# S5's tables with both parts side by side, modulation's loads first, the filters' second half later

## The chip, the core and the metric

The kernel runs on one core of a Trainium2 chip. Its engines work side by side and each in its own order: TensorE (PE) multiplies matrices, VectorE (DVE) and ScalarE (ACT) work element by element, GpSimd (POOL) gathers, SyncE (SP) issues most of the loads. The metric is the time of one execution on the device, in microseconds (us). Before the change it is 1788.65 us, the median of three runs (1786.26 to 1789.34).

## What is computed

One layer over 512 latent tokens of width 1024 and 256 tokens of context. A conditioning vector gives shifts, scales and gates (modulation). The normalised and modulated tokens go through one projection whose columns are split: 512 of them to S5 (32 groups of 16 channels, a complex diagonal state space in both directions, whose scans over the latents start from the context's last states), 1536 to Hyena (three streams, a convolution of width 3, and two long convolutions through spectra with filters that a small network makes). Both halves are joined and projected, and a retrieval of single-neuron experts (PEER) ends the layer.

```python
px = modulate(rmsnorm(x, g_norm1[l]), shx1, scx1) @ w_in[l] + b_in[l]
pc = modulate(rmsnorm(ctx, g_norm1[l]), shc1, scc1) @ w_in[l] + b_in[l]
...
lam_bar, b_bar = s5_discretise(...)            # b_bar = ((lam_bar - 1) / lam) * b
st_c = s5_states(uc, lam_bar, b_bar, None, dr == 1)
st_x = s5_states(ux, lam_bar, b_bar, h0, dr == 1)
y_x = y_x + s5_readout(st_x, s5_c_re[l, dr], s5_c_im[l, dr])
...
filt_x = hyena_filters(L, hf_w1, hf_b1, hf_wh, hf_bh, hf_freq, hf_wout, hf_decay)
z_x = hyena_mixer(px[..., S5_W:], hy_conv_w, hy_conv_b, filt_x, hy_d, rows)
mix_x = merge_head_groups(y_x, z_x, w_glu, b_glu, g_out_s5, g_out_hy, w_out)
x = x + gx1 * mix_x
x = x + gx2 * peer(modulate(rmsnorm(x, g_norm2), shx2, scx2), ...)
```

## The kernel before

The program is written as a sequence of stages for the Tile framework, whose scheduler then sets the order of the instructions on each engine; an engine runs its list strictly in that order. Two strings give the order in which the stages are written. EARLY orders the first loads on SyncE's queue: `h`, `f`, `s` are small tables, `w`, `t`, `d` the filters' output weights, the tables of sines and cosines and the decay rates, `x` the rows of x and of the context, `a0` to `a7` the eight blocks (1 MB each) of modulation's weights, `b` the S5 parameters. SEQ orders the work: `H` the filters' hidden layers, `A0` to `A3` (`filter_rows`, lines 507 to 534) the four filter groups, `B` their sums (536), `N` their norms (555), `k` and `K` their spectra (`filter_spectra`, 568), which go to the DRAM tile KD; `P0` to `P7` the products with modulation's weights (pmod, 426) and `M` the vectors made of them (modr, 431), `S` the norms of the rows of x, `X` and `C` the modulated x (xs, 443 to 446) and context; `U` and `u` the first four blocks of the projection for x and for the context (`s5_inputs`, `s5_context`, 653 and 665); `5` the S5 parameters (many small VectorE operations, most of 128x32). A product of two fp32 matrices is made of three matmuls of halves (lines 307 to 309), and the lower half of each block of weights (win0l to win15l, 303) is a subtraction of 128x1024 on VectorE.

After these comes S5 itself, in eight slices of four groups (SEQ has ended there). For each slice `added` (908) makes W, the input weights as complex products of powers (PB) and bb; turns them on TensorE (wt, WT, 930), and multiplies them with the inputs Ur (pv, VS). `states` (946) makes the turns E (586), turns VS by E (rt, VP), scans along time (H, 974) and turns back (ru, SF); `from_states` (993) makes C, the output weights, and multiplies SF by it (py, 1010). The complex product of two tables takes four multiplications, an addition and a subtraction, all through the helper at line 586. Hyena is written between the second and the third slice: projection blocks win4 to win15 with their convolutions (hq, uq, x2t), the spectra of the inputs (pu, pw, 1161, multiplied into spt and sp, 1163 to 1168), and back (pE, pY), until the inverse roots rz (487). Then the GLU, the output projection, the norms, and PEER.

Memory is held in pools. The filters and the S5 parameters share one pool (`ff`, line 340), which is closed when SEQ has ended (873); the pool of S5's slices (`fb`, 877) opens then and takes its place, so that a first write there waits for the last read of what lay there. In PSUM the tag of `ps5` has three banks, shared by the spectra of the filters (two banks a group), by wt, pv and py. The tag `sp` has four buffers, in which the filters' output weights and the tables trig lie, and later the spectra of the inputs.

## Time and profile before

| what | us |
|---|---|
| median of three runs | 1788.65 |
| the profiled execution | 1782.07 |
| its span | 1780.3 |
| TensorE busy in the span | 1670.0 (94%) |
| VectorE busy | 1491.0 (84%) |
| ScalarE busy | 817.9 (46%) |
| first matmul of the projection (px, win0) | 89.49 |
| first S5 row on VectorE (wt1w) | 162.24 |
| first product of the input spectra on VectorE (spt) | 280.99 |
| transposes behind the inverse roots (pyt) | 400.34 |
| first matmul of PEER's queries (pq) | 477.84 |

All times are counted from the start of the span. An engine that is idle is not by that the one to blame: what matters is which of them others wait for, and that differs from stretch to stretch.

### The profile page before, as it was taken

The page shows a single profiled execution, that of the slowest core. Times are in us where ns is not written, and L with a number is a line of the kernel's source. Part 1 is how long each engine was busy: PE and PEld are TensorE (multiplying, and loading weights), DVE is VectorE, ACT ScalarE, POOL GpSimd, SP SyncE. Part 2 cuts the span into 40 slices and gives each one's busy share as a digit, 9 for nine tenths or more (in the row PEclk, how much of TensorE's full clock was granted, in tenths as well). Part 3 has the DMA queues.
Part 4 walks back from the last instruction along what each step waited for, and adds up shares of the span by engine and source line. Part 5 has one row for each costly group of instructions (what it writes and reads, how often), then busy time and mean ns, then how long its engine had stood idle before and what let it go on. Part 6 is the DMA issues. An engine that isn't in the chain of part 4 may idle for free.

```text
span 1780.3 us, 24942 instructions
## 1 busy us (share of the span) xinstructions
PE 1670.0 (94%) x8731; PEld 1410.6 (79%) x8731; DVE 1491.0 (84%) x3039; ACT 817.9 (46%) x1616; POOL 169.5 (10%) x158
## 2 busy tenths in 40 slices
PE   5799998789899999998999989999999999999997
PEld 1477654456799999998999978877878788999996
DVE  7965989986688989989999958788878787888887
ACT  3443543234433323236989844444434344444444
POOL 0000000000000000001101101111111112222221
PEclk9899999899899999999999989999999999999999
DMA  9436453122444444446989899999999998999981
GB/s 372 155 98 209 156 170 91 51 75 71 124 156 139 141 147 151 145 147 246 330 319 333 322 321 387 385 356 378 363 353 358 357 339 320 342 327 349 335 311 71
DMA packets 170228, 436.13 MB, mean 245 GB/s; under 512 B 17139, under 2 KB 102004, under 8 KB 150902
## 3 DMA queue, kind: packets, MB, share of 16 engines
q1 hardware_dynamic: 128854, 251.28, 41.8%
q0 software_dynamic: 18432, 134.23, 20.5%
q10 hardware_dynamic: 22816, 49.03, 7.6%
q8 instruction: 69, 1.13, 0.3%
q14 instruction: 57, 0.47, 0.1%
HBM read 381.52 MB, written 52.92 MB: 244 GB/s over the span
## 4 chain that ended last, share of the span: by engine, by line
PE 63%; DVE 12%; issue 1%; ACT 1%; DMA 1%; ACTq 0%; DVEq 0%
PE pacc L308 9%; PE pacc L309 9%; PE pacc L307 9%; PE pa L309 7%; PE pa L307 7%; PE pa L308 7%; PE pgg L1566 5%; PE pq L309 2%; PE pq L307 2%; PE pq L308 2%; DVE idx L1352 1%; DVE rs L1350 1%; PE pg L1266 1%; DVE idx L1348 1%; PE po L307 1%
## 5 line engine op out<-in xcount | busy, mean ns | idle before, releaser
L308 PE MATMUL pacc<-vl,wwh 128*128 128x512 f32 x768 | 299.6, 391 | 1.8 <-DVE vl L1607 1.8
L309 PE MATMUL pacc<-vh,wwl 128*128 128x512 f32 x768 | 295.1, 390 | 0.0
L1430 POOL DMA_INDIRECT uvr<-in_uv_dram,gidx x128 | 157.1, 1228 | 1090.6 <-DVE accg L1439 764.6
L307 PE MATMUL pacc<-vh,wwh 128*128 128x512 f32 x768 | 238.3, 391 | 8.4 <-ACT vh L1606 8.4
L1607 DVE TENSOR_TENSOR vl<-vr,vh 128x1024 fp32r<-128x1024 f32 x128 | 155.3, 1219 | 26.8 <-ACT vh L1606 26.7
L307 PEld LDWEIGHTS pacc<-vh,wwh 128*128 128x128 f32 x768 | 143.5, 188 | 39.4 <-ACT vh L1606 11.3
L308 PEld LDWEIGHTS pacc<-vl,wwh 128*128 128x128 f32 x768 | 144.1, 188 | 33.6 <-DVE vl L1607 3.6
L309 PEld LDWEIGHTS pacc<-vh,wwl 128*128 128x128 f32 x768 | 144.2, 188 | 29.7
L1439 DVE SCALAR_TENSOR_TENSOR accg<-uvr,wgt,accg 128x1024 f32<-128x1024 f32 x128 | 163.7, 1279 | 4.1 <-ACT wgt L1436 1.8
L1431 DVE SCALAR_TENSOR_TENSOR junk<-uvr,hrow 128x1024 f32<-128x1024 f32 x128 | 155.9, 1218 | 0.0
L1606 ACT ACTIVATE vh<-vr 128x1024 fp32r<-128x1024 f32 x128 | 133.0, 1050 | 44.1 <-PE pacc L309 33.8
L1615 ACT ACTIVATE wwh<-gw 128x384 fp32r<-128x384 f32 x128 | 67.1, 524 | 185.4 <-PE pacc L308 146.1
L1616 DVE TENSOR_TENSOR wwl<-gw,wwh 128x384 fp32r<-128x384 f32 x128 | 70.9, 554 | 53.9 <-ACT wwh L1615 53.9
L1566 PE MATMUL pgg<-o,o 128*128 128x128 f32 x768 | 93.0, 278 | 4.3 <-ACT o L1562 4.3
L1566 PEld LDWEIGHTS pgg<-o,o 128*128 128x128 f32 x768 | 92.1, 194 | 4.5 <-ACT o L1562 4.5
L1557 DVE TENSOR_TENSOR o<-iotak,cols 128x512 f32<-128x512 f32 x96 | 65.8, 685 | 10.1 <-PE pgg L1566 10.1
L1564 DVE TENSOR_SCALAR o<-iotak,cols 128x128 f32<-128x128 f32 x240 | 70.1, 342 | 0.0
L1434 ACT ACTIVATE wgt<-dots 128x1 f32<-128x1 f32 x128 | 25.3, 198 | 93.1 <-DVE junk L1431 93.1
L1562 ACT ACTIVATE o<-o,cols 128x128 f32<-128x128 f32 x144 | 63.6, 493 | 0.0
L1369 ACT ACTIVATE ga<-pa 128x384 f32<-128x384 f32 x128 | 60.4, 472 | 2.4 <-DVE gw L1612 2.1
L1568 ACT ACTIVATE gst<-pgg 128x512 f32<-128x512 f32 x96 | 56.7, 591 | 1.2 <-PE pgg L1566 1.1
L1612 DVE TENSOR_TENSOR gw<-gal,gc 128x384 f32<-128x384 f32 x88 | 48.4, 553 | 7.4 <-DMA gal<-GA 5.5
(1812 smaller groups left out, 4133.9 us busy)
## 6 DMA issues: line engine op xcount, KB each, us to landing
vr<-in_uv_dram SPq DMA_DIRECT2D x128, 512.0 KB
GD<-gst ACTq DMA_DIRECT2D x12, 2048.0 KB
gc<-GD SPq DMA_DIRECT2D x32, 768.0 KB
GA<-ga ACTq DMA_DIRECT2D x88, 192.0 KB
gal<-GA SPq DMA_DIRECT2D x88, 192.0 KB
wb<-in_w_ada_dram SPq DMA_DIRECT2D x32, 512.0 KB
wa<-in_w_ada_dram SPq DMA_DIRECT2D x8, 1024.0 KB
KD<-kk SPq DMA_DIRECT2D x16, 256.0 KB
```

Source lines behind the costliest of these rows:

```text
L307: nc.tensor.matmul(o, a[0], b[0], start=start, stop=False)
L308: nc.tensor.matmul(o, a[0], b[1], start=False, stop=False)
L309: nc.tensor.matmul(o, a[1], b[0], start=False, stop=stop_)
L1430: GP.indirect_dma_start(out=uvr, out_offset=None, in_=I["uv"], in_offset=bass.IndirectOffsetOnAxis(ap=gidx[:, s:s + 1], axis=0))
L1431: ins = V.scalar_tensor_tensor(junk, uvr[:, 0:D], 1.0, hrow, ALU.mult, ALU.mult, accum_out=dots[:, s:s + 1])
L1439: V.scalar_tensor_tensor(accg, uvr[:, D:2 * D], wgt[:, s:s + 1], accg, ALU.mult, ALU.add)
L1564: last = V.tensor_scalar(o1[:, e], iotak, cols[:, 0, t:t + 1], cols[:, 2, t:t + 1], ALU.is_equal, ALU.mult)
L1566: mm = PE.matmul(pg[:, e, :], o2[:, e], o1[:, e], start=True, stop=True)
L1606: A.activation(vh, vr, AF.Copy)
L1607: (V if QUIET or i >= P - VLV else GP).tensor_tensor(vl, vr, vh.bitcast(F32), ALU.subtract)
L1615: A.activation(wh, gw, AF.Copy)
L1616: last = V.tensor_tensor(wl, gw, wh.bitcast(F32), ALU.subtract)
```

## The change

Two strings change, four groups of tables, and the pools.

- EARLY: the small tables, then modulation's weights, with the S5 parameters behind `a2` and x behind `a3`; the filters' tables and decay rates behind `a7`.
- SEQ: the S5 parameters first, then modulation's products one behind the other, `M`, and the first filter group; the spectra of the second order of the filters (k2, k3, K2, K3), before the context's `U3`, now end the sequence. A new part `W` writes W of slices 0 and 1 and E of slice 0 there.
- Tables: b, c and the finer factor of E are kept as (-im, re, im) or (im, re, -im) side by side. A complex product then is one multiplication of the real part of the powers by two neighbouring parts, one of the imaginary part by the two before, and one addition, each twice as wide. c comes so from the host; for b and E three negations on ScalarE make the third part. H is made in place of VP.
- Pools: the filters' pool lies on the right side, the parameters' pool apart from it, closed by `W`; S5's early tables (W, CM, the temporaries q2) take that one's place, and the main ones (VS, R, E, rt, SF, C, WT, YC) that of the filters' pool. WT of slices 0 and 1 and E of slice 0 take buffers of the tag `sp`.

What the diff changes in `columns` and `gates_r` stands behind RGATE, which is 0 in both programs.

```diff
@@ -53,8 +53,8 @@
-EARLY = "h f s t1 t0 x1 x0 w0 a0 d0 a1 a2 w1 a3 a4 a5 d1 a6 a7 x2 b d2 d3"
-SEQ = "H P0 S0 A0 P1 B0 k0 P2 A1 P3 B1 P4 P5 P6 P7 M X0 N0 k1 S2 K0 X1 K1 U0 C0 A2 B2 U1 C1 5 u0 u1 A3 U2 u2 B3 N1 k3 k2 K3 U3 K2 u3"
+EARLY = "h f s a0 a1 a2 b a3 x1 x0 a4 a5 a6 a7 t1 w0 d0 t0 w1 d1 x2 d2 d3"
+SEQ = "H 5 P0 P1 P2 S0 P3 P4 P5 P6 P7 M A0 X0 B0 X1 A1 S2 k0 B1 N0 k1 K0 C0 U0 K1 C1 U1 A2 u0 u1 B2 A3 W U2 B3 u2 N1 U3 u3 k2 k3 K2 K3"
@@ -339,19 +338,24 @@
-    fpool = ff.enter_context(tc.tile_pool(name="ff", bufs=1))
+    fpool = ff.enter_context(tc.tile_pool(name="fl", bufs=1, side="right"))
+    fe_ = ExitStack()
+    epool = fe_.enter_context(tc.tile_pool(name="fe", bufs=1))
@@ -671,6 +676,147 @@
+    b3 = sm("b3", [P, G5, 3, 16])
+    EB3 = sm("EB3", [P, G5, 3, 8])
...
+    def both_parts(o, pw, x3, g0, name):
+
+        t = (q2(name + "1"), q2(name + "2"))
+        for e in range(2):
+            tt(t[e], pw[e][:, :, g0:g0 + GS].rearrange("p j g -> p g j").unsqueeze(3).broadcast_to((P, GS, T8, 32)),
+               x3[:, g0:g0 + GS, 1 - e:3 - e].rearrange("p g e h -> p g (e h)").unsqueeze(2).broadcast_to((P, GS, T8, 32)), ALU.mult)
+        tt(o.rearrange("p e g j h -> p (g j) e h"), *(x.rearrange("p g j (e h) -> p (g j) e h", h=16) for x in t), ALU.add)
...
+        WT = sm(f"WT{s_}", [P, 2, GS, P], tag="sp", bufs=4) if s_ < NEARLY else sl(f"WT{s_}", [P, 2, GS, P], tag="WT", bufs=1)
...
+        for e in range(2):
+            tt(t[e].rearrange("p (g a n) -> p g a n", g=GS, n=16), EA_[e][:, gs].unsqueeze(3).broadcast_to((P, GS, A8, 16)),
+               EB3[:, gs, 1 - e:3 - e].rearrange("p g e b -> p g (e b)").unsqueeze(2).broadcast_to((P, GS, A8, 16)), ALU.mult)
+        tt(E.rearrange("p e g (a b) -> p (g a) e b", b=8), *(x.rearrange("p (q e b) -> p q e b", e=2, b=8) for x in t), ALU.add)
...
+        H, t2 = v3(f"H{s_}", "rt", 2), v3(f"rt2{s_}", "rt", 2)
+        tt(H, VS, both(E[:, 0]), ALU.mult)
+        tt(t2, VS, both(E[:, 1]), ALU.mult)
+        tt(H[:, 0], H[:, 0], t2[:, 1], ALU.add)
+        tt(H[:, 1], H[:, 1], t2[:, 0], ALU.subtract)
@@ -712,6 +858,14 @@
+        elif part[0] == "W":
+            fe_.close()
+            fb_ = ExitStack()
+            pools5[0] = fb_.enter_context(tc.tile_pool(name="fb1", bufs=1))
+            for s_ in range(NEARLY):
+                weights(s_)
+                if s_ < NEARLY - 1:
+                    turns(s_)
@@ -853,17 +1003,17 @@
+            cmul((b3[:, :, 1], b3[:, :, 2]), (bc_h(fr_), bc_h(fi_)), (gh(bre), gh(bim)), (gh(bt1), gh(bt2)))
+            for x in (b3, c3):
+                A.activation(*((x[:, :, 0], x[:, :, 2]) if x is b3 else (x[:, :, 2], x[:, :, 2])), AF.Copy, scale=-1.0)
@@ -873,151 +1023,18 @@
+    pools5[1] = fb_.enter_context(tc.tile_pool(name="fb2", bufs=1, side="right"))
...
-        t1, t2 = q2(f"ct1{s_}"), q2(f"ct2{s_}")
-        pr, pi = (pw4(x, g0, GS) for x in PC)
-        cr, ci = (x4(gh(cre[:, e]), g0, GS) for e in range(2))
-        tt(t1, pr, cr, ALU.mult)
-        tt(t2, pi, ci, ALU.mult)
-        tt(C[0], t1, t2, ALU.add, FG)
-        tt(t1, pi, cr, ALU.mult)
-        tt(t2, pr, ci, ALU.mult)
-        tt(C[1], t1, t2, ALU.subtract, FG)
```

What this does to the order, first on TensorE at the last two groups of the filters' spectra (pke and pko, from hfb). Before, they end where the projection block win4 begins:

```order
L576 MATMUL pke_1206<-hfb_1034,trig_97 128x256 x4
L576 MATMUL pko_1207<-hfb_1034,trig_97 128x256 x4
L576 MATMUL pke_1256<-hfb_632,trig_97 128x256 x4
L308 MATMUL pc_1274<-cs_601,win3h 128x256
L309 MATMUL pc_1274<-cs_601,win3l 128x256
L307 MATMUL pc_1274<-cs_601,win3h 128x256
L308 MATMUL pc_1274<-cs_601,win3h 128x256
L309 MATMUL pc_1274<-cs_601,win3l 128x256
L307 MATMUL px_1681<-xs_412,win4h 128x512
L576 MATMUL pko_1257<-hfb_632,trig_97 128x256 x4
L308 MATMUL px_1681<-xs_414,win4h 128x512
L309 MATMUL px_1681<-xs_412,win4l 128x512
```

After, the last two (from hfb_901 and hfb_1040) stand behind the whole of win8, and the first pv of S5 right behind them:

```order
L307 MATMUL px_1885<-xs_540,win8h 128x512
L308 MATMUL px_1885<-xs_538,win8l 128x512
L581 MATMUL pke_1372<-hfb_901,trig_100 128x256 x4
L581 MATMUL pko_1373<-hfb_901,trig_100 128x256 x4
L581 MATMUL pke_1390<-hfb_1040,trig_100 128x256 x4
L1152 MATMUL pz_1854<-ident,uq_1851 128x128 x4
L439 MATMUL modr0T<-ident,modr_1868 128x98 x2
L581 MATMUL pko_1391<-hfb_1040,trig_100 128x256 x4
L439 MATMUL modr0T<-ident,modr_1868 128x98 x2
L646 MATMUL pmodr_1925<-wb_0_0_1927,sc 1x512 x2
L764 MATMUL pv_1422<-Ur,WT_1106 128x96 x4
L764 MATMUL pv_1430<-Ur,WT_1106 128x96 x4
```

What moved: five blocks of the projection, with their convolutions' transposes (pz) and the later modulation (pmodr), from behind the last spectrum to ahead of it.

A little ahead of that on TensorE in the changed program stands the second of the four groups (pke_1354 and pko_1355, from hfb_1039), whose two halves are set apart by 14 rows of the projection; the copies WT of slice 1 on ScalarE come behind the last reads of trig_101 by this group:

```order
L583 ACTIVATE kev_1364<-pke_1354 128x512
L1155 ACTIVATE uw<-pz_1800 128x4x128
L1139 ACTIVATE hp_1845<-px_1820,small 128x512
L1141 ACTIVATE hq_1847<-px_1820,cbq,small 128x512
L738 ACTIVATE WT_1150<-wt_1151 128x512
L738 ACTIVATE WT_1150<-wt_1157 128x512
L301 ACTIVATE win9h<-win9r 128x1024
L1139 ACTIVATE hp_1910<-px_1885,small 128x512
L1141 ACTIVATE hq_1912<-px_1885,cbq,small 128x512
L583 ACTIVATE kev_1382<-pke_1372 128x512
L583 ACTIVATE kev_1400<-pke_1390 128x512
```

On VectorE, the place where S5 begins. Before, W of slice 0 (wt1w) follows the last rows of the spectra (kk):

```order
L581 TENSOR_TENSOR kk_1218<-kev_1216,pko_1207 128x512
L581 TENSOR_TENSOR kk_1221<-kev_1216,pko_1207 128x512
L303 TENSOR_TENSOR win5l<-win5r,win5h 128x1024
L581 TENSOR_TENSOR kk_1268<-kev_1266,pko_1257 128x512
L581 TENSOR_TENSOR kk_1271<-kev_1266,pko_1257 128x512
L586 TENSOR_TENSOR wt1w_1332<-PB_868,bb 128x512
L586 TENSOR_TENSOR wt2w_1333<-PB_869,bb 128x512
L586 TENSOR_TENSOR wt1w_1391<-PB_868,bb 128x512
L586 TENSOR_TENSOR wt2w_1392<-PB_869,bb 128x512
L586 TENSOR_TENSOR et_1449<-EA_880,EB_882 128x384
L586 TENSOR_TENSOR et_1449<-EA_881,EB_883 128x384
L586 TENSOR_TENSOR WBrw_1330<-wt1w_1332,wt2w_1333 128x512
```

After, the last kk are followed by C and H of slice 0; W, E and the products ct for C have been made earlier:

```order
L1148 TENSOR_TENSOR uq_1916<-hq_1912 128x256
L1149 TENSOR_TENSOR uq_1916<-hq_1912 128x256
L586 TENSOR_TENSOR kk_1384<-kev_1382,pko_1373 128x512
L586 TENSOR_TENSOR kk_1387<-kev_1382,pko_1373 128x512
L586 TENSOR_TENSOR kk_1402<-kev_1400,pko_1391 128x512
L586 TENSOR_TENSOR kk_1405<-kev_1400,pko_1391 128x512
L651 TENSOR_TENSOR mod<-modr0T,small 128x4 x4
L591 TENSOR_TENSOR C_1455<-ct_1456,ct_1457 128x32x2x16
L591 TENSOR_TENSOR H_1464<-VS_1421,E_1119 128x768
L591 TENSOR_TENSOR rt_1465<-VS_1421,E_1119 128x768
L591 TENSOR_TENSOR H_1464<-H_1464,rt_1465 128x384 x2
L302 TENSOR_TENSOR win10l<-win10r,win10h 128x1024
```

What moved: 34 rows of VectorE's list more stand ahead of the first S5 row that the filters' memory holds back, among them W of two slices, E of one, and four more blocks win.

## Rows read from the trace of the kernel before

**Rows 1.** Busy time of each engine by stretch; columns in its first line.

```profile
core 0: us, PE busy (x) PEld busy (x) DVE busy (x) ACT busy (x) POOL busy (x), PEclk, DMA share, GB/s
0.00:50.00 50.00, 29.66 (x120) 12.30 (x120) 38.98 (x182) 17.90 (x38) 0.70 (x6) 0.93 0.90 348
50.00:89.49 39.49, 29.57 (x150) 15.70 (x149) 37.95 (x91) 17.58 (x31) 0.00 (x0) 0.91 0.49 154
89.49:162.24 72.75, 70.59 (x374) 57.24 (x372) 36.48 (x67) 28.75 (x46) 0.00 (x0) 0.98 0.42 127
162.24:280.99 118.75, 111.97 (x639) 72.78 (x636) 107.86 (x189) 59.13 (x124) 1.95 (x10) 0.99 0.55 177
280.99:400.34 119.35, 95.08 (x483) 56.29 (x481) 113.46 (x197) 35.32 (x84) 1.23 (x6) 0.93 0.24 63
400.34:477.84 77.50, 69.05 (x289) 49.82 (x289) 52.23 (x73) 36.81 (x62) 0.95 (x1) 0.90 0.38 112
477.84:1780.00 1302.16, 1264.05 (x6687) 1146.42 (x6687) 1104.02 (x2245) 622.45 (x1232) 164.64 (x135) 0.99 0.79 281
```

**Rows 2.** Chain of waits, 369 to 400 us: start, length, what.

```profile
369.54 0.94 DVE H L974
...
376.01 3.72 PE pY L1189 x16
...
384.42 3.47 PE pY L1189 x16
...
394.88 0.70 DVE x2t L1195
...
400.34 1.13 PE pyt L1227 x4
```

**Rows 3.** VectorE in order of time, 340 to 350 us: start, length, operation.

```profile
340.87 0.95 DVE L586 TENSOR_TENSOR rt<-VS,E 128x768 f32<-128x768 f32 x1
341.73 0.68 DVE L586 TENSOR_TENSOR wt1w<-PB,bb 128x512 f32<-128x512 f32 x1
342.34 0.68 DVE L586 TENSOR_TENSOR wt2w<-PB,bb 128x512 f32<-128x512 f32 x1
342.94 0.68 DVE L1163 TENSOR_TENSOR spt<-pu,sp 128x512 f32<-128x512 f32 x1
...
348.59 0.99 DVE L586 TENSOR_TENSOR et<-EA,EB 128x384 f32<-128x384 f32 x2
349.50 0.68 DVE L1167 TENSOR_TENSOR sp<-spt,spt 128x512 f32<-128x512 f32 x1
```

**Rows 4.** Loads of wa: shortest/median/longest ns, first and last start in us.

```profile
L360 SPq DMA_DIRECT2D wa<-in_w_ada_dram x8: 328/328/762, 4.8 to 28.5; - x8
```

**Rows 5.** Copy of pmod and first load's row on VectorE, in order of time.

```profile
8.40 0.18 DVE L600 TENSOR_SCALAR ex<-small 128x32 f32<-128x32 f32 x1 [5.89 <-DMA small<-in_small_dram]
...
55.36 0.68 DVE L431 COPY modr<-pmod 98x512 f32<-98x512 f32 x1
```

**Rows 6.** TensorE in order of time at three places.

```profile
89.49 0.58 PE L307 MATMUL px<-xs,win0h 128*128 128x512 f32 x1
...
154.78 1.67 PE L576 MATMUL pko<-hfb,trig 128*128 128x256 f32 x7
...
156.75 0.39 PE L307 MATMUL px<-xs,win4h 128*128 128x512 f32 x1
156.98 0.40 PE L308 MATMUL px<-xs,win4h 128*128 128x512 f32 x1
...
278.97 1.55 PE L1161 MATMUL pu<-uw,fwd 128*128 128x512 f32 x3 [1.29 <-DMA fwd<-in_fwd_dram]
```

**Rows 7.** VectorE in order of time, 155 to 163 us.

```profile
155.55 1.23 DVE L303 TENSOR_TENSOR win5l<-win5r,win5h 128x1024 fp32r<-128x1024 f32 x1 [2.01 <-ACT win5h L302]
156.70 1.28 DVE L581 TENSOR_TENSOR kk<-kev,pko 128x512 f32<-128x512 f32 x2
162.24 0.69 DVE L586 TENSOR_TENSOR wt1w<-PB,bb 128x512 f32<-128x512 f32 x1 [4.27 <-DMA KD<-kk]
```

**Rows 8.** VectorE's waits, 86 to 163 us: total, times, longest.

```profile
DVE win4l L303 <- ACT win4h L302: 8.5, 1, 8.5
DVE kk L581 <- issue: 6.2, 1, 6.2
DVE wt1w L586 <- DMA KD<-kk: 4.3, 1, 4.3
```

**Rows 9.** VectorE in order of time at 281 us.

```profile
280.99 0.69 DVE L1163 TENSOR_TENSOR spt<-pu,sp 128x512 f32<-128x512 f32 x1 [1.39 <-PE pu L1161]
```

More of the change, by code (lines that the diff above doesn't have):

```diff
@@ L65 @@
 NYU = 2
-NW = 2
+NEARLY = 2
 NF4 = 4
@@ L97 @@
 NOO = 3
-S5M = 1
 HYAT = 2
@@ L384, in build @@
         elif what[0] == "b":
-            for e, t in enumerate((bre, bim, cre)):
-                early(t, I["bc"][:, e] if e < 2 else I["bc"][:, 2:4])
+            for e, t in enumerate((bre, bim)):
+                early(t, I["bc"][:, e])
+            early(c3, I["c3"])
         elif what[0] == "w":
```

284 lines of the change are left out of this document (139 added, 145 removed).

## The prediction, made before the changed kernel ran

> **What bounds the kernel now.** I read the busy time of the engines in stretches first [rows 1], with the cuts at the places where the kernel changes hands. The last stretch, from the first product of the queries at 477.84 us to the end, is 1302 of the 1780.3 us; the change touches nothing that lives there (its edits of the gates stand behind a switch that is off in both programs). What can move the time is when that stretch begins. Ahead of it lie six stretches: VectorE is nearly full in the second (37.95 of 39.49 us), has half of the third to spare (36.48 of 72.75), while TensorE is full there (70.59), is full again in the fourth (107.86 of 118.75) and above all in the fifth (113.46 of 119.35, TensorE at 95.08). The chain of waits [rows 2] says the same of the fifth: it goes back over H, the products of the spectra and the pY matmuls, alternately VectorE and TensorE, to the inverse square roots behind which the GLU starts at 400.34. From 400.34 to 477.84 both programs have one order of instructions, so I carry those 77.5 us over unchanged. The question is thus: when does that row at 400.34 come?
>
> **Loads first.** Before, the eight blocks of modulation's weights are issued up to 28.5 us, behind the filters' tables, and the copy of the finished sums stands at 55.4 [rows 4, 5]. After, twelve megabytes (8.4 of the weights, 2.1 of x, 1.3 of S5's parameters, the small table) stand ahead of or at the last block. At the 348 GB/s of the first 50 us [rows 1] that is 34.5 us, plus the 8.4 us at which the first load frees VectorE [rows 5]: the copy comes at about 43, some 12 us sooner. Little of it arrives at the first projection (89.49) [rows 6], because VectorE is in the way: what it must do before that projection is the same list in both orders, less 0.3 us (the S5 parameters and W of slice 0 take the place of two filter groups), it was busy 76.9 us in the first 89.5 [rows 1], and it can't start before 8.4. That allows no earlier than 84 to 85. And the filters' decay rates now land behind the weights, at about 46; ScalarE's row that takes their absolute value stands ahead of the rows that modulate x, so these begin at 46 too and not at 43, with 36.6 us of VectorE's list still to run, and some waits for TensorE's transposes. I take 86.5 (84 to 91): a gain of 3.
>
> **Tables with both parts side by side.** A table of W or C cost six operations of 128x512 and costs three of 128x1024; one of E six of 128x384 and now three of 128x768. On a full VectorE what counts is the distance from start to start, not the shown duration: 0.60 for 128x512, 0.46 for 128x384, 0.86 for 128x768 [rows 3], 1.15 for 128x1024 [rows 7]. So a table of W or C falls from 3.60 to 3.45, one of E from 2.76 to 2.58, about 0.2 each with the unrounded starts; 24 tables make 4.7 us. The shown durations (0.68 and 1.23) would give more, 0.13 a pair. [...] The three negations added go to ScalarE, which is half idle there (17.58 of 39.49).
>
> **The filters' second half moved back.** This is the edit that costs. TensorE's rows between the first projection and the last spectrum were worth 63.1 us by the spacing of their kinds, and took 66.6 (89.49 to about 156.1, where the last one starts) [rows 6]. In the new order the last spectrum stands behind 119 more matmuls of the projections (0.23 each, 27.1), 14 more of the later modulation (4.9), 12 more of the spectra's own (5.2; these stood ahead of the first projection), W's edges and transposes for two slices with those of the first convolutions (5.2), and a little else: 105.9. With the same factor of 1.055 they take 111.7, to 198.2.
>
> This matters because the pool of S5's main tables (VS, R, SF, C, H) takes the memory of the filters' pool. Before, the first S5 row on VectorE waits 4.3 us for the last write of the filters' results to DRAM and starts at 162.24, six behind the start of the last spectrum [rows 6, 7]. After, the same wait stands ahead of C and H of slice 0: 198.2 + 6 = 204.2, and about 2 more, because H waits for VS, which ScalarE can only copy then. I take 206, against 162.24. Against that stands what now lies ahead of it: W of slices 0 and 1 (6.8), E (2.6), ct (2.3), four more splits of projection weights (4.5), five groups of short convolutions (9.7), the rest small: 27.2 us of VectorE's list. So VectorE does 36.5 + 27.2 = 64 us in the 119 from 86.5 to 206 and idles 55; before it idled 36 in the third stretch, mostly behind TensorE and the write [rows 8]. The moved work fills half of what the later start opens.
>
> **From there to the first product of the spectra** (280.99 [rows 9]) VectorE's list falls from 106.4 to 61.6. Before, 106.4 took 118.75, a factor of 1.116, with TensorE's 104.1 in step beside it. After, TensorE's list is 63.1 against 61.6, as evenly matched, so I keep the factor: 68.7, to 274.7. Without any loss it is 268, with the 1.18 that TensorE shows there (104.1 in the 122.9 to 278.97 [rows 6]) 279.
>
> **From there to the inverse roots** VectorE's list was 111.6 and took 119.35 (1.069). After, only three slices' states are done by then, and not four, which leaves 124.4 (the saving of the tables is in it). At a factor of 1.05 that is 130.6, to 405.3; with 1.013 and 1.069 on either side, 126 and 133. So the 6 us gained up to the first product are spent, and more: the work done early is less than the slice that moved behind.
>
> **The sum.** 405.3 against 400.34 is 5 us later. On the profiled execution (1782.07, span 1780.3) that is 1787; that execution lies 6.6 below the median of the runs shown, 1788.65, to which I add the difference: 1794. A difference of about 0.2% (3.6 us) is what a measurement of this kernel can tell from none.
>
> **Rivals.** *A gapless S5 (faster).* W, E and C of the first slices are ready when the filters end, so S5 could run without the waits of the fourth stretch. First projection at 84, last spectrum at 195.7, S5 at 201.7, 61.6 x 1.02 to 264.5, 124.4 x 1.013 to 390.5: 10 sooner, 1779. For it: in the fifth stretch VectorE loses only 6 of 119. Against: TensorE has 63.1 of its own in that stretch, and the two feed each other. It decides from a first product of the spectra before 268. *The edits cancel.* Projection at 85, the tables save the shown durations (0.13 a pair, 72 pairs, 9.4 us, so 4.7 more than I count), or the factor in the fourth stretch is 1.05: 400 +- 3.5, thus 1789. [...] *A late end of the filters (slower).* The second half's spectra are chained: the transposes of W of slice 1 wait in two of the three PSUM banks of their tag until ScalarE may copy them, which by the order it does only behind the second of the four groups (their memory is a trig table's until then), so the first two groups have one bank for their two halves, and go TensorE, ScalarE, TensorE, VectorE in turn. If one of those turns is late, TensorE stands with the projections behind it. At 6 us for each of the two (VectorE's longest wait ahead of kk is 6.2 in [rows 8]) S5 starts at 218, and with 68.7 and 133 behind it the roots come at 420: +19, 1808. *That the change doesn't do what it says:* the loads are in fact reordered in the program, so only its effect on the first projection can fail; it is in the 84 to 91.
>
> **How the numbers follow.** Forecast (+5, its own range +1 to +12): 0.42. Cancels (-3.5 to +3.5): 0.23. Gapless: 0.20. Late filters: 0.15. Of the forecast's 0.42 some 0.12 lies within 3.6 us of no change, of the gapless case 0.02, and 0.04 of the cancelling case falls out on the fast side. That gives faster 0.22, same 0.33, slower 0.45. The range of eight in ten reaches into the gapless case (-7) and into the late one (+17): 1782 to 1806.
>
> **What would show it.** In the changed profile: the copy of modulation's sums at about 43 (if it is at 50 or later, the loads are not what I think); the first projection at 84 to 91; the last sum of the spectra on VectorE at about 200, and C and H of slice 0 right behind a wait for the write to DRAM at 202 to 208, with VectorE under 60% busy from 90 to there; the first product of the spectra at 270 to 279; the row at 400.34 at 400 to 410; and the queries 77.5 behind it. Consecutive 128x1024 rows of W and C should start 1.15 apart. I would be wrong if S5's first H came well before the last spectrum (then the memory is not what it waits for), or if VectorE had no idle time between 90 and 200.

## The result, and the profile after

The changed kernel takes 1805.08 us (median of four runs, 1803.64 to 1807.4), the kernel before 1787.45 on the same chip: 1.0108 of it, with a 95% interval of 1.0091 to 1.0126. By the ratio that is 19 us more; the two medians lie 17.6 us apart. The profiled execution took 1804.69 us, its span is 1802.9. The time lies within the range that was given (1782 to 1806), at its upper end; the forecast itself, 5 us slower, was too small by a factor of almost four.

The busy time by stretch in the profile after, cut at the rows that [rows 1] is cut at (columns in the first line); the fourth cut is the first S5 row that waits for the filters' memory:

```profile
core 0: us, PE busy (x) PEld busy (x) DVE busy (x) ACT busy (x) POOL busy (x), PEclk, DMA share, GB/s
0.00:50.00 50.00, 25.64 (x118) 5.74 (x119) 41.62 (x205) 12.92 (x28) 0.70 (x6) 0.83 0.89 348
50.00:99.47 49.47, 40.69 (x128) 20.51 (x128) 40.34 (x71) 26.77 (x52) 0.31 (x1) 0.62 0.40 128
99.47:215.40 115.93, 115.05 (x637) 89.42 (x636) 61.58 (x106) 46.21 (x80) 0.62 (x2) 1.00 0.47 148
215.40:284.60 69.20, 64.79 (x354) 41.29 (x353) 62.56 (x83) 37.04 (x74) 0.74 (x5) 1.00 0.58 196
284.60:419.77 135.17, 102.76 (x527) 63.77 (x525) 126.21 (x190) 39.25 (x95) 1.58 (x8) 0.89 0.22 53
419.77:498.09 78.32, 67.45 (x289) 48.74 (x289) 52.35 (x74) 36.69 (x62) 0.95 (x1) 0.94 0.37 111
498.09:1802.90 1304.81, 1263.28 (x6688) 1145.08 (x6687) 1105.14 (x2245) 624.18 (x1232) 165.96 (x135) 0.99 0.80 281
```

From the inverse roots to the queries it is 78.3 us (77.5 before), behind them 1304.8 (1302.2): 3 of the 22.6 us by which the two spans differ. The other 19.4 are there when the row at 400.34 in [rows 1] comes at 419.77. Up to it VectorE was busy 332 us (334.7 before) and idle 87 (65.6 before). The loss is idle time of VectorE: 5 us more of it ahead of the first projection, 18 more between that and the first S5 rows, where TensorE is full (115.05 of 115.93) as in the third stretch of [rows 1], 4 less from there to the first product of the spectra, and 3 more behind that.

What the prediction had not seen stands ahead of the first projection. TensorE in order of time in the profile after (start, length, operation, in brackets the idle time before it and what ended it):

```profile
64.92 3.14 PE L646 MATMUL pmodr<-wb,sc 128*1 128x512 f32 x8 [2.43 <-DMA wb<-in_w_ada_dram]
68.00 2.07 PE L526 MATMUL pf<-hwo,hid 64*128 64x256 f32 x4
...
73.52 1.87 PE L646 MATMUL pmodr<-wb,sc 128*1 128x512 f32 x4 [1.24 <-DMA wb<-in_w_ada_dram]
...
83.08 1.87 PE L646 MATMUL pmodr<-wb,sc 128*1 128x512 f32 x4 [2.93 <-DMA wb<-in_w_ada_dram]
...
90.65 3.11 PE L581 MATMUL pke<-hfb,trig 128*128 128x256 f32 x8
...
96.12 1.97 PE L581 MATMUL pke<-hfb,trig 128*128 128x256 f32 x8
...
99.47 0.58 PE L306 MATMUL px<-xs,win0h 128*128 128x512 f32 x1
```

The last modulated block of x starts at 70.8 us (88.2 before), but the first projection starts at 99.47 (89.49 before [rows 6]). In between TensorE works down its list: the later modulation, which waits four times for its weights (6.9 us in all), the filters' products pf, and two groups of spectra. The same eight pke take 3.11 us at 90.65 and 1.97 at 96.12: the granted clock is 0.62 from 50 to 99.5. In the 50 us ahead of that it is 0.83 (0.93 before [rows 1]), and there TensorE was busy 25.64 us (29.66 before) and waited 10.1 us for modulation's weights.

The later modulation and its waits are not what is new there: in the kernel before, 28 rows of it (32 after) stand ahead of the first projection too, and wait 8.3 us for their loads. New is what the rows take. Everything up to the first projection, before and then after:

```profile
0.00:89.49 89.49, 59.23 (x269) 28.00 (x269) 76.93 (x272) 35.48 (x69) 0.70 (x6) 0.92 0.72 262
0.00:99.47 99.47, 66.34 (x244) 26.24 (x245) 81.96 (x275) 39.69 (x79) 1.02 (x7) 0.73 0.65 238
```

TensorE has 25 rows fewer and is busy 7 us longer, at a granted clock of 0.73 and not 0.92. With the mean time that each kind of row took before, the list after would take 54 us (an estimate, with cT counted as xT); the 12 us above that go with the lower clock.

Where S5 begins, VectorE in order of time:

```profile
207.23 1.29 DVE L586 TENSOR_TENSOR kk<-kev,pko 128x512 f32<-128x512 f32 x2 [2.14 <-PE pko L581]
208.43 0.36 DVE L651 TENSOR_TENSOR mod<-modr0T,small 128x4 f32<-128x4 f32 x4
215.39 1.23 DVE L591 TENSOR_TENSOR C<-ct,ct 128x1024 f32<-128x1024 f32 x1 [6.59 <-DMA KD<-kk]
217.63 0.96 DVE L591 TENSOR_TENSOR H<-VS,E 128x768 f32<-128x768 f32 x1 [1.02 <-ACT VS L769]
```

This is [rows 7] fifty-three us later: the wait for the write to DRAM is there, 6.6 and not 4.3 us, and behind it the short one for VS.

### The profile page after: what moved, and what is told of

Read it like the earlier page. It is cut to its first block, busy times and chain, and to the rows that moved or that the text cites. A ratio compares the mean times of both kernels' runs of the same rounds, so it can differ in the third digit from the quotient of the medians.

```text
span 1802.9 us, 24884 instructions
## 1 busy us (share of the span) xinstructions
PE 1679.7 (93%) x8731; PEld 1414.5 (78%) x8731; DVE 1489.8 (83%) x2967; ACT 823.1 (46%) x1620; POOL 170.9 (9%) x158
## 4 chain that ended last, share of the span: by engine, by line
PE 62%; DVE 11%; DMA 1%; issue 1%; ACT 1%; ACTq 0%; DVEq 0%; SPq 0%
PE pacc L307 10%; PE pacc L308 9%; PE pacc L306 9%; PE pa L308 7%; PE pa L306 7%; PE pa L307 7%; PE pgg L1578 5%; PE pq L308 2%; PE pq L306 2%; PE pq L307 2%; DVE idx L1370 1%; DVE rs L1368 1%; PE pg L1284 1%; DVE idx L1366 1%; DVE val L1365 1%
## 5 line engine op out<-in xcount | busy, mean ns | idle before, releaser
L1448 POOL DMA_INDIRECT uvr<-in_uv_dram,gidx x128 | 158.4, 1238 | 1090.3 <-DVE accg L1457 744.4
L306 PE MATMUL pacc<-vh,wwh 128*128 128x512 f32 x768 | 243.4, 391 | 10.8 <-ACT vh L1621 10.8
L1457 DVE SCALAR_TENSOR_TENSOR accg<-uvr,wgt,accg 128x1024 f32<-128x1024 f32 x128 | 163.7, 1279 | 5.3 <-ACT wgt L1454 3.3
```

The lines of the kernel that those rows point to most:

```text
L306: nc.tensor.matmul(o, a[0], b[0], start=start, stop=False)
L1448: GP.indirect_dma_start(out=uvr, out_offset=None, in_=I["uv"], in_offset=bass.IndirectOffsetOnAxis(ap=gidx[:, s:s + 1], axis=0))
L1457: V.scalar_tensor_tensor(accg, uvr[:, D:2 * D], wgt[:, s:s + 1], accg, ALU.mult, ALU.add)
```

## The experiments

The table has all runs, with the profiles' times: the first projection, the last sum of the filters' spectra (kk), the first product of the input spectra (spt), VectorE's idle time up to that, its busy time from there to the inverse roots, and the inverse roots (rz on VectorE, which starts within 0.1 us of the row at 400.34 in [rows 1]; that row is a transpose that starts with the roots and not behind them). Ratios are to the kernel before, on the same chip each. A profile is one execution: e11 and e17 are the same kernel, and their columns up to spt differ by 3 to 5 us, while from spt to the roots both take 114.9.

| run | ratio, interval | projection | last kk | spt | idle to spt | busy behind | roots |
|---|---|---|---|---|---|---|---|
| before | 1 | 89.5 | 157.3 | 281.0 | 59.7 | 113.4 | 400.3 |
| changed | 1.0108 (1.0091 to 1.0126) | 99.5 | 207.8 | 284.6 | 78.5 | 126.3 | 419.9 |
| e1 old loads and stages | 1.0097 (1.0070 to 1.0124) | 97.0 | 190.4 | 291.7 | 74.1 | 114.5 | 414.8 |
| e2 old loads | 1.0056 (1.0036 to 1.0077) | 108.6 | 196.2 | 279.3 | 69.5 | 121.4 | 410.8 |
| e3 one W early | 1.0045 (1.0029 to 1.0061) | 99.5 | 181.6 | 288.3 | 66.7 | 110.0 | 410.1 |
| e4 later modulation late | 1.0132 (1.0107 to 1.0157) | 87.5 | 200.5 | 298.5 | 76.4 | 111.1 | 421.1 |
| e5 tables alone | 1.0022 (1.0011 to 1.0033) | 85.6 | 158.4 | 281.0 | 58.9 | 109.4 | 404.2 |
| e6 e1 with one W early | 1.0006 (0.9991 to 1.0021) | 96.5 | 161.8 | 284.4 | 51.9 | 99.2 | 393.4 |
| e7 new order, one pool, none early | 1.0058 (1.0037 to 1.0080) | 95.3 | 167.3 | 282.6 | 65.9 | 115.5 | 408.6 |
| e8 none early | 1.0068 (1.0045 to 1.0091) | 99.8 | 180.8 | 289.2 | 71.0 | 113.5 | 414.3 |
| e9 two W early, no E | 1.0088 (1.0064 to 1.0113) | 99.4 | 186.3 | 291.8 | 73.0 | 113.4 | 416.8 |
| e10 one W and E early | 1.0104 (1.0080 to 1.0128) | 99.2 | 187.0 | 290.0 | 72.2 | 114.0 | 417.0 |
| e11 e2 with one W early | 0.9993 (0.9979 to 1.0007) | 103.5 | 169.0 | 282.6 | 55.8 | 103.5 | 397.5 |
| e12 e1 with one W and E early | 1.0011 (0.9997 to 1.0025) | 98.1 | 163.7 | 287.3 | 54.5 | 99.4 | 398.3 |
| e13 e3 with idle matmuls | 1.0046 (1.0032 to 1.0061) | 103.5 | 181.4 | 288.5 | 67.9 | 111.6 | 408.2 |
| e14 changed with idle matmuls | 1.0128 (1.0106 to 1.0150) | 95.4 | 209.3 | 288.2 | 81.3 | 126.1 | 426.0 |
| e15 e11 with idle matmuls | 1.0047 (1.0033 to 1.0062) | 111.3 | 177.2 | 288.7 | 61.4 | 104.0 | 404.0 |
| e16 e3 with mixed loads | 1.0023 (1.0013 to 1.0032) | 103.0 | 173.2 | 279.5 | 60.3 | 112.2 | 403.1 |
| e17 e11 again | 0.9983 (0.9971 to 0.9996) | 107.7 | 173.7 | 286.2 | 59.3 | 103.5 | 401.1 |

**The order of loads and stages put back (e1).** The theory after the result was still the prediction's: the order moves the filters' second half, and that costs.

```diff
-EARLY = "h f s a0 a1 a2 b a3 x1 x0 a4 a5 a6 a7 t1 w0 d0 t0 w1 d1 x2 d2 d3"
-SEQ = "H 5 P0 ... B2 A3 W U2 B3 u2 N1 U3 u3 k2 k3 K2 K3"
+EARLY = "h f s t1 t0 x1 x0 w0 a0 d0 a1 a2 w1 a3 a4 a5 d1 a6 a7 x2 b d2 d3"
+SEQ = "H P0 S0 A0 ... u0 u1 A3 W U2 u2 B3 N1 k3 k2 K3 U3 K2 u3"
```

> The changed kernel with the two strings of before (loads and stages in the old order; the early W stands behind the last filter group), tables and pools as changed. If the order of loads and stages is what costs, nearly all of the 19 us comes back and the narrower tables' 4 to 5 us show: 1782 to 1787, first projection at 88 to 91. If the pools are what costs (S5's main tables in the filters' memory, WT in the buffers of the trig tables), it stays at 1795 or above, with S5's first C behind the write to DRAM later than 185 us.

1803.07 us: both strings back, and hardly anything is won. The filters end at 190 here, against 157 before, so it is not the strings alone that put their second half behind the projections. The theory fell.

**The loads alone put back (e2).** Only the EARLY line of e1.

> The changed kernel with the old order of the first loads alone (the filters' tables ahead of modulation's weights), stages, tables and pools as changed. If the late filter tables are what holds the first projection at 99.5 us, it comes at 89 to 92 and the time falls by 7 to 10, to about 1796. If TensorE's rows of the later modulation hold it (16 of them stand ahead of it in this order too), it stays at 97 or later and the time within 4 us of 1805.

1796.26, 9 us won, but not by the way that was expected: the first projection comes later still (108.6), with more of the filters done ahead of it: the scheduler lays out TensorE's order anew with EARLY, and 20 rows of pf and 32 of the spectra more stand there.

**One slice early (e3).**

```diff
-NEARLY = 2
+NEARLY = 1
```

> The changed kernel with only slice 0's W early (W of slice 1 and E of slice 0 come later, so no second WT waits for the buffer of a trig table). In the order the last spectrum of the filters then stands behind 125 matmuls of the projections and not 216. If that wait is what moves the filters' end, the last sum of the spectra comes at about 180 and not 208, S5's C at 187, and the time falls by 5 to 12, to 1793 to 1800. If VectorE's whole list decides, what is taken out of the idle time comes back behind it and the time stays within 4 us of 1805.

1793.88, 11 us won, with the first projection where it was (99.5). The filters end at 181.6. Busy times of e3 from the first projection to the last sum, to the spectra's first product, to the roots:

```profile
99.50:182.30 82.80, 81.92 (x452) 65.88 (x451) 45.10 (x77) 33.43 (x57) 0.31 (x1) 1.00 0.44 134
182.30:288.30 106.00, 101.27 (x598) 69.14 (x597) 94.35 (x135) 57.09 (x119) 1.78 (x9) 0.98 0.57 181
288.30:410.10 121.80, 94.15 (x468) 56.72 (x467) 110.03 (x165) 31.67 (x73) 0.93 (x5) 0.93 0.24 62
```

Here, as before and after the change, TensorE is full first and VectorE half idle (37.7 of 82.8), then both are nearly full, then VectorE is. What VectorE has left at the third cut, 110 us, was 126 in the changed kernel.

**The later modulation taken out of the first projection's way (e4).** Its first four pieces are written among the Hyena blocks.

```diff
@@ s5_context
-        more_modulation()
@@ hyena, for ct in range(12)
             more_modulation()
+            if ct % 3 == 0:
+                more_modulation()
```

> The changed kernel with the first four pieces of the later modulation (rows pmodr, loads wb) written among the Hyena blocks and not behind the context's projection, so that none of their 16 matmuls and no wait for their loads stands ahead of the first projection on TensorE. If those waits hold the first projection, it comes at 86 to 91 and the time falls by 8 to 12, to about 1795. If the filters' rows on VectorE and the lower clock of TensorE hold it, it comes at 95 or later and the time stays within 4 us of 1805.

The first projection comes at 87.5 as expected, 12 us sooner, and the kernel takes 1809.27, no less than the changed one. Busy times of e4, from the start to the first projection, to the last sum, to the spectra's first product, to the roots:

```profile
0.00:87.50 87.50, 50.83 (x192) 23.26 (x192) 77.78 (x268) 36.85 (x74) 1.02 (x7) 0.71 0.57 217
87.50:201.20 113.70, 110.87 (x603) 85.32 (x604) 60.18 (x100) 45.02 (x79) 0.62 (x2) 0.98 0.43 137
201.20:298.50 97.30, 87.19 (x497) 56.43 (x497) 84.12 (x119) 48.92 (x102) 1.33 (x8) 0.96 0.63 200
298.50:421.10 122.60, 93.92 (x467) 56.37 (x466) 111.06 (x165) 32.15 (x73) 0.87 (x5) 0.91 0.24 62
```

Ahead of the first projection TensorE now does 50.8 us of work and not 66.4, in a time in which it has some to spare; that work (16 rows of the spectra among it), and 7.0 us of waits for loads, stand behind it, the waits in the third stretch, where TensorE and VectorE both are nearly full (87.19 and 84.12 of 97.30), and the first product of the spectra comes 14 us later than in the changed kernel. The roots come 1 us later, since VectorE has 111 us left behind that product and not 126. So the first projection is no milestone: it says nothing without the work that TensorE has done by then.

**Tables alone, and the two changes apart (e5 to e8).** e5 is the kernel before with the new tables; e6 is e1 with one early W; e7 has the new order with one pool and nothing early; e8 is the changed kernel with nothing early.

```diff
@@ e5 (with the old strings) and e7 (with the new ones)
-    fpool = ff.enter_context(tc.tile_pool(name="fl", bufs=1, side="right"))
-    epool = fe_.enter_context(tc.tile_pool(name="fe", bufs=1))
+    fpool = ff.enter_context(tc.tile_pool(name="ff", bufs=1))
+    epool = fpool
...
-    pools5[1] = fb_.enter_context(tc.tile_pool(name="fb2", bufs=1, side="right"))
+    pools5[0] = pools5[1] = fb_.enter_context(tc.tile_pool(name="fb", bufs=1))
@@ e5, e7, e8: NEARLY = 0; e6: NEARLY = 1 with the strings of e1
```

> The kernel before with the tables side by side alone: old order of loads and stages, one pool for filters and parameters and one behind it for S5, no table early. By the prediction's term (0.15 to 0.2 us a table on a full VectorE, 24 tables) it is 4 to 5 us faster than before, 1781 to 1783; by what VectorE's busy time up to the inverse roots fell in the changed kernel (334.7 to 332.4) 2 to 3 us, 1784. If the tables themselves cost something (wider operations, more of ScalarE), it is at 1787 or above.

> The changed kernel with the old order of loads and stages and only slice 0's W early. It differs from the run with the old order and both slices early in that one number. If the buffers and banks that WT of slice 1 and E hold are what made that run slow (last sum of the spectra at 190 us there), the filters end at 155 to 165 here, S5's C or W begins by 170 and the time is 1778 to 1788. If the split of the pools is what costs, it stays at 1795 or above.

> The changed kernel's order of loads and stages with one pool and no table early: the order alone, with the new tables. If the order costs by itself (first projection at 97 to 100, spectra behind more of the projections), it is 5 to 10 us above before, at 1791 to 1796. If only the early tables cost, it is within 4 us of the tables alone, 1781 to 1787.

> The changed kernel with no table early, pools split and order as changed. Against the run with one slice early (1794) it tells what slice 0's early W is worth: by the prediction's idle time of VectorE behind the filters W of a slice (3.4 us) done early saves at most that, so 1794 to 1798 here; if early tables only take away banks and buffers, it is below 1792.

The tables alone make the kernel slower, not faster: 1788.25, 1.1 to 3.3 parts in a thousand. VectorE's busy time up to the roots does fall, from 334.7 to 331.4 us, but where it falls nothing waits for it. (TensorE's order changes a little with the tables: 24 rows of the spectra fewer stand ahead of the first projection.) VectorE in e5 behind the last product of the spectra, which is done at the same time as before (373.8 and 373.6):

```profile
375.71 0.76 DVE L590 TENSOR_TENSOR ru<-ru,ru 128x256 f32<-128x256 f32 x2
378.49 0.43 DVE L1204 TENSOR_TENSOR yy<-eo 128x256 f32<-128x256 f32 x1 [2.02 <-ACT eo L1202]
...
382.02 0.69 DVE L484 TENSOR_TENSOR rzl<-zsq,rzh 128x512 fp32r<-128x512 f32 x1 [1.52 <-ACT rzh L483]
384.83 0.69 DVE L1053 TENSOR_TENSOR YC<-YC,pk 128x512 f32<-128x512 f32 x1 [2.11 <-PE pk L1050]
...
390.96 1.29 DVE L1111 TENSOR_TENSOR catl<-catz,cath 128x512 fp32r<-128x512 f32 x2 [1.84 <-PE pY L1200]
...
404.24 3.35 DVE L491 RECIPROCAL rz<-rzq 128x512 f32<-128x512 f32 x1 [0.22 <-ACT rzq L490]
```

S5's last rows are through at 377 us and what is left is the chain of [rows 2], pY on TensorE, eo on ScalarE, yy and catl on VectorE, in which each waits for the next: 30.4 us here, 26.7 before. The time saved came out as waits in that chain. Part of them goes with TensorE's clock. The first eight pY of the chain, before and then in e5, and the busy times of the chain in the same order:

```profile
373.76 1.99 PE L1189 MATMUL pY<-inv,sp 128*128 128x256 f32 x8 [1.57 <-DVE sp L1167]
373.93 3.78 PE L1200 MATMUL pY<-inv,sp 128*128 128x256 f32 x8 [6.34 <-DVE sp L1178]
```

```profile
373.60:400.32 26.72, 22.35 (x132) 17.09 (x132) 21.25 (x41) 12.84 (x22) 0.00 (x0) 0.96 0.28 86
373.60:404.24 30.64, 26.59 (x132) 19.87 (x132) 18.44 (x34) 12.69 (x22) 0.00 (x0) 0.84 0.21 70
```

In e5 TensorE has been idle for 6.3 us when the chain begins and runs the same eight matmuls in nearly twice the time; its 132 rows take 4.2 us more, at a granted clock of 0.84 and not 0.96. That is about as much as the chain grew, in one profile of each kernel; no run changes this clock alone.

e6 against e1 settles what made e1 slow. From the first projection to the last sum and to the spectra's first product, e6 first, then e1:

```profile
96.50:162.50 66.00, 63.98 (x353) 52.59 (x352) 38.50 (x69) 29.68 (x52) 0.31 (x1) 0.97 0.34 100
162.50:284.40 121.90, 114.73 (x708) 80.65 (x707) 110.14 (x155) 62.84 (x129) 1.89 (x10) 1.00 0.61 193
```

```profile
97.00:191.10 94.10, 90.51 (x487) 70.22 (x486) 49.92 (x82) 39.54 (x70) 0.62 (x2) 0.96 0.42 126
191.10:291.70 100.60, 91.24 (x519) 62.41 (x518) 84.28 (x121) 47.42 (x94) 1.16 (x7) 0.95 0.60 188
```

With one W early the filters end 28 us sooner, VectorE idles 27.5 and not 44.2 us in the first of these stretches, and is at 1785.85 no slower than the kernel before; with W of slice 1 and E early (e1) it is 16 us slower by the ratios; in the new order the same two tables cost 11 (e3 against the changed kernel). In e6's profile the roots stand 7 us ahead of those before, and the time is no shorter: the stretch behind the queries, the same instructions in all these kernels, takes 1302.5 us in the profile before and 1308.0 in this one, and why is not known. So the ratio decides, and not the roots. e7 and e8 put the new order without early tables at 1.006 to 1.007; whether the pools are split (e8) or not (e7) makes no difference that the intervals show. One W early is worth 3 us in the old order (e6 against e5) and 4 in the new (e3 against e8), in both within the intervals.

**Which of the early tables (e9, e10), and what the order costs (e11, e12).** WT and E of the early slices lie in the tag of four buffers that hold two tables of the filters' output weights and the two trig tables, so the third early one has to wait for a trig table. e9 and e10 each make two early tables.

```diff
+NEARLY_E = 0        # e9, with NEARLY = 2; e10: NEARLY = 1, NEARLY_E = 1
...
-                if s_ < NEARLY - 1:
+                if s_ < NEARLY_E:
                     turns(s_)
```

> The changed kernel, order as changed, with W and WT of two slices early but not E of slice 0: two early tables take the two buffers of the filters' output weights, none that of a trig table. In the order the last spectrum stands behind 140 matmuls of the projections (216 as changed). If the third table, which has to wait for a trig table while its transposes hold two PSUM banks, is the cause, the last sum of the spectra comes at 178 to 188 and the time is 1791 to 1798. If the work of slice 1 done early is the cause (TensorE's transposes, VectorE's W ahead of the filters' rows), it stays at 1802 to 1807.

> The changed kernel, order as changed, with W and E of slice 0 early but nothing of slice 1: again two early tables and no trig buffer. By the third table's wait: 1791 to 1798, last sum of the spectra at 178 to 190. If E early is the cause (its buffer is free only when the last filter group has read its weights, and it keeps two temporaries of W busy until then), 1800 to 1807.

1800.44 and 1803.57. The end of the filters does come at 186 to 187, as the third table's wait would have it; but the time does not follow, since the spectra's first product comes at 290 to 292, later than in the changed kernel. So in the new order the third table explains when the filters end, 21 us of it, and not the loss: two early tables cost 8 and 10 us over one, a third little more. The theory fell as an account of the time there; why a second table costs that much is not settled. In the old order it is the other way round. e12 has W and E early and is at 1.0011, no dearer than e6 within the intervals; the third table, W of slice 1, takes it to e1's 1.0097, 15 us, and the last sum from 163.7 to 190.4. There the third table's wait fits the end of the filters and the time, but no run tells that wait from the work of slice 1 itself.

e11 has the old loads, the new stages and one W early; e12 the old loads and stages and W and E of slice 0 (NEARLY = 1, NEARLY_E = 1 on e1).

> The changed kernel with the old order of loads, the new order of stages, and one slice's W early. With one slice early the new loads and stages gave 1794 and the old ones 1786. If it is the loads that make these 8 us, this run is at 1784 to 1788 with TensorE at 0.86 or more of its clock before the first projection; if it is the stages, at 1792 to 1796.

> The changed kernel with the old loads and stages, and W and E of slice 0 early: the old order with as much early as takes no trig buffer. By VectorE's idle time of 28 us between the first projection and the filters' end there (one W early: 1786), E early moves 2.6 us of its work into it: 1782 to 1785, a little better than before and the changed kernel. If VectorE's work left behind the spectra does not fall, 1785 to 1788.

e11 is at 1783.51 and e3, which differs in EARLY alone, at 1793.88. So with one W early the stages in the new order cost nothing (e6, with the old stages, is at 1.0006), and the new loads cost 9 to 11 us by the ratios (e11 and e17 against e3); with all tables early they cost 9 (e2 against the changed kernel). With all tables early the new stages are even 7 us better than the old ones (e2 against e1, with intervals that just overlap). The new loads with the old stages were not run. e12 is at 1786.77, where the second half of its expectation had it: VectorE's work behind the spectra did not fall (99.4 us, 99.2 in e6).

**What it is in the loads (e13 to e17).** Three things differ: TensorE's granted clock before the first projection (0.71 in e3, 0.92 in e11), that the filters' tables land behind modulation's weights, and TensorE's order (in e11, 20 rows of pf and 32 of the spectra more stand ahead of the first projection). e13, e14 and e15 add idle matmuls ahead of the blocks of x and of the filters' products, five ahead of each of 16: the traces have 80, where the expectations say 60; e16 moves the tables of the filters forward between modulation's weights; e17 is e11 again.

```diff
@@ modulated, for x (e13, e14, e15); the same ahead of pf in the first two filter groups
             pp = psa(f"{name}T{k}")
+            for i in range(5 if name == "x" else 0):
+                PE.matmul(pp[:, 0:256], ones.bitcast(BF16)[:, 0:P], ones.bitcast(BF16), start=True, stop=True)
@@ e16 (with NEARLY = 1)
-EARLY = "h f s a0 a1 a2 b a3 x1 x0 a4 a5 a6 a7 t1 w0 d0 t0 w1 d1 x2 d2 d3"
+EARLY = "h f s a0 a1 a2 t1 w0 d0 b a3 x1 x0 a4 t0 w1 d1 a5 a6 a7 x2 d2 d3"
```

> The run with one slice early and the new order (1794, granted clock 0.71 before the first projection, that one at 99.5 us) with 60 idle matmuls more: five of 128x256 in bf16 ahead of each of the eight transposed blocks of x and of the first filter groups' eight products, into banks that are written over; nothing else. If the low clock is what the new loads cost (TensorE's 66.8 busy us before the first projection for a list that the old loads run at 0.89 to 0.92), the clock rises to 0.85 or more, the first projection comes 5 to 8 us sooner and the time falls by 4 to 8, to 1786 to 1790. If waits for loads and filter rows hold TensorE there, the time stays within 3 us of 1794 or rises by the idle matmuls' own time.

> The same 60 idle matmuls in the changed kernel itself (1805, clock 0.73 before the first projection). If the clock there costs, the time falls by 4 to 8, to 1797 to 1801, the end of the filters moving with the first projection. If VectorE's work left behind the spectra decides alone, the time stays within 4 us of 1805.

> The same idle matmuls in the run with the old loads, the new stages and one slice early (1783.5, clock 0.92 before the first projection already). Where the clock is granted anyway, they can only take TensorE's time: 60 matmuls of 0.1 to 0.2 us, partly in its idle 36 us, so 1782 to 1788. If they help here too by more than 3 us, what they help with is not the clock.

> The new order of stages and one slice early, as in the runs at 1794 (new loads) and 1783.5 (old loads), but with the first filters' output weights, tables and decay rates loaded behind the third block of modulation's weights and the other tables behind the fifth; modulation's first blocks stay ahead. If it is when the filters' tables land that costs in the new loads, the time is that of the old loads, 1782 to 1787, with 24 of the filters' matmuls pf and 16 of the spectra ahead of the first projection in TensorE's order. If modulation's weights first are what costs (their late neighbours on the queue, the clock), 1790 to 1796.

> The run with the old loads, the new stages and one slice early once more, on the chip of the run above: 0.9993 of before by the first comparison (0.9979 to 1.0007). If it is faster than both kernels at all, it is so by 1 to 4 us here; otherwise it is the kernel before's equal.

Busy times from 44 us to the first projection (in e13 to 1.5 us behind it), e13 and then e3:

```profile
44.00:105.00 61.00, 46.70 (x217) 27.83 (x217) 50.91 (x109) 30.21 (x55) 0.31 (x1) 0.82 0.38 128
```

```profile
44.00:99.50 55.50, 44.39 (x155) 22.45 (x147) 46.43 (x97) 29.36 (x54) 0.31 (x1) 0.63 0.40 131
```

The idle matmuls raise the clock from 0.63 to 0.82 and the time stays (1793.56 against 1793.88), with the first projection 4 us later and not sooner. In the changed kernel that row comes 4 us sooner, at 0.84 of the clock up to there and not 0.73, and the time is 1811.0 (1.0128 against 1.0108, which the intervals don't separate); in e15, the control, with the clock at 0.91 (0.92 in e11, 0.90 in e17), it is 1794.4, 10 us more. The control says that they are dear, 8 to 11 us of TensorE's busy time before the first projection (67.6 in e11, 70.6 in e17, 78.6 in e15), 0.10 to 0.14 us for each of the 80 where the expectation took 0.1 to 0.2, against 4.4 in e13 (66.8 in e3, 71.2). That the other 4 to 7 are what the clock gave back is an inference from these differences.

e16, with the tables forward, is at 1788.73, between its two expectations, and has more clock (0.83) without idle matmuls. Up to the first product of the spectra it has the same rows on TensorE as e3, kind by kind. e3 and then e16, from the start to that product:

```profile
0.00:288.30 288.30, 250.00 (x1290) 161.35 (x1291) 221.66 (x486) 130.20 (x254) 3.10 (x17) 0.89 0.56 187
0.00:279.50 279.50, 242.77 (x1290) 160.42 (x1291) 219.20 (x486) 127.79 (x252) 3.10 (x17) 0.93 0.58 193
```

The same 1290 rows take 7.2 us less at the higher clock, and the product comes 8.8 us sooner. By the ratios e16 is 4 us faster than e3, with intervals that just overlap, out of the 9 to 11 between e3 and e11 or e17. What is left is 5 to 7 us, and there clock and order differ together: e11 and e17 are at 0.92 and 0.90 of the clock before the first projection, and they have four slices of S5 through their last product (py) by the spectra's first, where e3 and e16 have three. Which of the two it is stays open.

e17 is the one version here that is faster than both kernels, by 0.4 to 2.9 parts in a thousand of the kernel before (1782.9 us); e11, the same kernel, does not show it by itself (0.9979 to 1.0007). It has the new tables, the new stages and one W early, and the old loads.

## Why the prediction was wrong

**What bounds, right.** The rows of [rows 1] from the queries on moved by 3 us, and the loss stands ahead of the inverse roots. The tail that was carried over at 77.5 us is 78.3.

**The loads, right up to the copy and wrong from there.** The copy of modulation's sums was put at 43 us and came at 44.1. The first projection was put at 86.5 and came at 99.5: this is the term of the sum that failed. It was worked out from VectorE's list alone, as if that held the row; the last block of the modulated x started at 70.8. What held the projection was TensorE's own list, and that was so before already: there TensorE works without a gap from 83.0 us into the first projection, which waits for nothing. The prediction had looked at that list for the filters' end and not for the beginning, and it had no term for TensorE's clock. With the new loads the list ahead of the projection, 25 rows shorter, took 66.3 us and not 59.2, at 0.73 of the clock and not 0.92; the 12 us that go with the lower clock by the estimate above are nearly all of the 13. That the time follows the first projection one for one was wrong too: in e4 the row comes 12 us sooner and the time is no shorter, in e2 it comes 9 us later and the time is 9 us shorter.

**The tables, right by the row and worth nothing.** Rows of 128x1024 start 1.14 us apart where 1.15 was said; VectorE's busy time up to the roots fell by 2.4 us in the changed kernel and 3.3 in e5, where 4.7 was said. None of it reached the end, and e5 is 4 us slower. The prediction took it off the list behind the first product as if VectorE's list alone set that stretch, though [rows 2] shows a chain in which the three engines alternate, and in e5 TensorE, behind 6.3 us of idle time, went through that chain at 0.84 of the clock and not 0.96.

**The filters' second half, right in the sum, wrong in the cause.** From the first projection to the start of the last spectrum 111.7 us were said and it is 107.3 (its last row starts at 206.8); C comes 8.6 us behind that, where 8 were said. From C to the first product of the spectra 68.7 were said and 69.2 are measured, from there to the roots 130.6 and 135.2 (126.3 busy where the list said 124.4, 9.0 idle where 6 were said). Added: 13 us for the projection, 3.5 less to S5, 0.5 and 4.6 behind, 14.5 us in all between 405.3 and 419.8. But the prediction laid the later end on the new order of the stages. The runs lay it on the early tables beyond one W (11 us in the new order, 16 in the old) and on the loads (9 to 11); the order of the stages costs nothing (e11, e17). The prediction had counted W of two slices and E as work moved into idle time, at no price of their own. And VectorE's waits in the third stretch, which it put mostly on TensorE and the write, have ScalarE's win4h as the longest in [rows 8] (8.5 us).

**The time to the first product.** It was to come 6 us sooner and came 3.6 later, and this could have been read beforehand from TensorE: up to that row it was busy 241.8 us and idle 39.2 before [rows 1], and 246.2 and 38.4 after. Its list up to there is nearly the same in both orders (1275 rows before, 1231 after), so the row can come sooner only by as much as TensorE's idle time or those 44 rows allow; the prediction let it come sooner by taking a better factor. What could not be read beforehand is that the shorter list takes longer: the clock up to there is 0.96 before and 0.90 after.

**The rival of the late filters** gave S5 at 218, the spectra at 287, the roots at 420 and 1808, all close to the profile (215.4, 284.6, 419.8), but by a mechanism that is not there: TensorE did not stand still between the first projection and S5 (0.9 us idle in 115.9). The 12 us lie ahead of the first projection. What the third table's wait does in the new order is to leave the last spectrum behind more rows of the projections (e9, e10), and the forecast had counted those. Numbers that fit don't show a cause.

## What to carry to other kernels

Where one engine is full in a stretch and another in the next, ask of each edit how much of the second one's list is done by the time the first lets go, and how much idle time the first has ahead of that; a row in between, such as a first projection, can move by 12 us and change nothing. Work that is made early takes buffers and places in the queues from what it is put ahead of (a third early table put the filters' end 21 us later): try it one table at a time, since here one W early was worth 3 to 4 us, hardly more than the intervals, and the two tables beyond it cost 11. And a saving on a busy engine is worth only what the chain behind it can take up (in e5 VectorE was busy 3.3 us less and the kernel took 4 us more). A list that is shorter in rows can be longer in time (here 244 rows took 66.3 us at 0.73 of the clock, and 269 took 59.2 at 0.92): compare the granted clock of a stretch before and after, ahead of the counts.

## What the runs showed of the hardware

TensorE's granted clock before the first projection was 0.71 to 0.78 in the runs with modulation's weights first, the filters' tables behind all of them and no idle matmuls, and 0.86 to 0.92 with the old loads (e16, between them, 0.83). Up to the first product of the spectra the same 1290 rows of TensorE took 250.0 us in e3 and 242.8 in e16, at 0.89 and 0.93 of the clock. In e5, behind 6.3 us of idle time, eight pY took 3.78 us; before, behind 1.6 us, the same eight took 1.99. With eighty matmuls of 128x256 in bf16 that have no use, the clock before the first projection was 0.84 in e13, where e3 has 0.71, and the time was the same (1793.56 and 1793.88); with the old loads, where it was 0.90 and 0.92 without them (e17 and e11) and 0.91 with them (e15), TensorE was busy 8 to 11 us longer up to that row and the kernel lost 10.
